# A convolution in Winograd form: the casting load of the last image pair split into 7, 65, 24 and 32 partitions

## Chip, core and metric

One core of one Trainium2 chip. The metric is the device time of one execution in microseconds (us); the median of the repeated runs is given, with lowest and highest in brackets. A ratio is the mean time of one kernel's fast runs over the mean of the other kernel's fast runs of the same rounds, so it is not quite the ratio of the medians quoted. The profiles name the engines of the core: PE multiplies matrices, DVE, ACT (ScalarE) and GpSimd (POOL) compute on elements, SP here only issues DMAs. A DMA is carried out by 16 DMA engines, which move packets and end each DMA with small completion packets (for the casting load of the kernel before 144 packets: 128 rows, and 16 of 4 bytes that take 9 ns in the median). The straggler, or late engine, is the DMA engine that ends last.

## The reference

A 3x3 convolution with padding 1, float32 in and out:

```python
batch, c_in, h, w, c_out = 16, 64, 64, 64, 128
x_pad = np.pad(x, ((0, 0), (0, 0), (1, 1), (1, 1)))
output[b, co] += weight[co, ci, kh, kw] * x_pad[b, ci, kh:kh+h, kw:kw+w]   # over ci, kh, kw
```

## The kernel before

Two images of 64 channels fill 128 partitions, so there are 8 pairs; each is 128 rows of 16 KB in float32. Seven pairs are loaded by plain DMAs from the SP queue into float32 tiles and cast to float16 by ScalarE or GpSimd. The last pair is cast during its load by one DMA from the GpSimd queue, the only queue in the kernel that casts. Each output pair is stored by two DMAs of 2 MB, the last pair by four of 1 MB.

Cut to the loads and stores, with some lines joined and `...` for what is left out:

```python
    def load(p):                                   # SP queue, float32
        xf[p] = next_slot([128, H, W], "xf")
        for lo, hi in cuts if p == 0 else [(0, H)]:
            keep(nc.sync.dma_start(
                    xf[p][:, lo:hi, :], x_rows[128 * p : 128 * p + 128, lo:hi, :]))
    ...
    def load_cast(p):                              # GpSimd queue, float32 -> float16
        xs[p] = xpool.tile([128, H, W], F16, tag="xc", name="xc")
        keep(nc.gpsimd.dma_start(xs[p], x_rows[128 * p : 128 * p + 128, :, :]))
    ...
    for p in range(NP):                            # NP = 8, NH = 7
        ...                                        # row sums of pair p + 1 on GpSimd
        if p == 0:
            for q in range(NH, NP):
                load_cast(q)
        for blk in range(4):
            ...                                    # matmuls, additions
            if blk in parts:                       # stores, SP queue
                for b2 in range(2):
                    keep(nc.sync.dma_start(out_rows[2 * p + b2, :, lo:hi, :], ...))
```

Of the kernel before, what the change touches and what calls it, by code (L numbers as in the profile page):

```python
# [13 lines left out]
def kernel(  # L14
# [6 lines left out]
    nc = tc.nc  # L21
# [6 lines left out]
    keep = tc.keep_in_program_order  # L28
    x_rows = x.rearrange("b c h w -> (b c) h w")
# [23 lines left out]
    xf, xs = {}, {}  # L53
# [23 lines left out]

    def load_cast(p):
        xs[p] = xpool.tile([128, H, W], F16, tag="xc", name="xc")
        keep(nc.gpsimd.dma_start(xs[p], x_rows[128 * p : 128 * p + 128, :, :]))  # L80

    for p in range(NH):
        load(p)
# [51 lines left out]
    for p in range(NP):  # L135
# [7 lines left out]
# [3 lines that stand above are left out]
# [92 lines left out]
```

## Time and profile before

| | before |
|---|---|
| time | 128.05 us (127.88 to 128.25, 3 runs) |
| span of the profiled execution | 126.0 us |
| last matmul / last addition end | 111 us / 113 us |
| bytes moved | 49.72 MB, of which 1.05 MB (as written) by the casting load |

The page of the profile has a line of 40 slices for each engine and for the DMA. The DMA line says how busy the engines were, and the GB/s line how much they moved: in the kernel after, at 24 us, the packets of the large loads took 904 ns in place of 624 and the DMA share stayed at 1.01, so an engine whose packets got longer still counts as busy. The stretch in which the casting load runs is shown here, as windows (columns: window, its length, busy us of PE, PE loads, DVE, ACT and GpSimd with instruction counts, granted clock, DMA share of 16 engines, GB/s as written), for the kernel before:

```profile
24.00:32.00 8.00, 8.00 (x76) 3.98 (x74) 6.46 (x11) 7.52 (x10) 2.47 (x2) 1.00 1.02 318
32.00:38.00 6.00, 6.00 (x60) 3.09 (x58) 4.58 (x8) 4.68 (x8) 4.21 (x2) 1.00 1.00 419
```

In the first window the rate is 318 GB/s at full share. That is no loss: half of the packets are cast rows (107 of 209), which read 16 KB and write 8 KB, and only what is written is counted (1.05 MB for the 128 rows; the page gives 17.07 MB read from HBM, which is all of the input in float32, 16.78 MB, and the weights). In the second the cast is nearly over and the rate is back.

### The profile page before, as it was taken

How to read it: one execution, taken by the hardware profiler on the slowest of the kernel's cores; microseconds unless marked ns; L12 is line 12 of the kernel's file. 1: busy time of each engine (PE TensorE's matmuls, PEld its weight loads, DVE VectorE, ACT ScalarE, POOL GpSimd, SP SyncE). 2: the span in 40 equal slices, each digit the busy share in tenths (PEclk: the TensorE clock that was granted, in tenths of full speed). 3: DMA queues.
4: the chain of work that ended last, by engine and by line, in shares of the span. 5: the costliest groups of instructions: out<-in, count | busy, mean ns of one | idle time of the engine just before them, and what ended most of it. 6: DMA issues, size and time to landing. Idle time of an engine off the chain costs nothing.

```text
span 126.0 us, 2439 instructions
## 1 busy us (share of the span) xinstructions
PE 106.0 (84%) x978; PEld 53.4 (42%) x978; DVE 84.4 (67%) x135; ACT 61.7 (49%) x94; POOL 33.6 (27%) x23
## 2 busy tenths in 40 slices
PE   0479999999999999999999999999999999940000
PEld 0334455545554545454545454555445544510000
DVE  0186777877777778777877787778777787770000
ACT  4184889998869896666333333333333333300000
POOL 2000297940661157005800480039000000000000
PEclk9999999999999999999999999999999999999555
DMA  4999999999999999999999999999999999999960
GB/s 122 304 431 443 427 426 426 348 320 317 393 432 427 429 429 427 421 432 421 437 437 416 442 416 432 437 421 421 432 421 437 437 416 442 413 406 437 429 265 13
DMA packets 4330, 49.72 MB, mean 395 GB/s; under 512 B 480, under 2 KB 480, under 8 KB 1120
## 3 DMA queue, kind: packets, MB, share of 16 engines
q1 hardware_dynamic: 4176, 48.53, 91.8%
q0 software_dynamic: 144, 1.05, 4.0%
q8 instruction: 7, 0.11, 0.3%
q14 instruction: 3, 0.02, 0.0%
HBM read 17.07 MB, written 33.55 MB: 402 GB/s over the span
## 4 chain that ended last, share of the span: by engine, by line
PE 82%; DMA 4%; DVE 2%; issue 1%; DVEq 0%; SPq 0%
PE acc L176 82%; DMA xf<-in_x_dram 4%; DVE ot L196 1%; DVE ss L98 1%; DVE ot L199 0%; DVEq L233 0%; SPq L51 0%; DVEq L196 0%
## 5 line engine op out<-in xcount | busy, mean ns | idle before, releaser
L176 PE MATMUL acc<-xs,Wt 64*128 64x504 f16 (+3 forms) x672 | 77.9, 379 | 0.0
L176 PEld LDWEIGHTS <-Wt 64*128 64x128 f16 x960 | 52.3, 95 | 53.7 <-issue 3.7
L196 DVE TENSOR_TENSOR ot<-acc,ut 128x512 f32<-128x512 f32 x64 | 41.3, 687 | 21.9 <-PE acc L176 19.0
L190 ACT COPY ut<-acc 128x512 f32<-128x512 f32 x64 | 34.4, 590 | 43.6 <-issue 39.0
L199 DVE TENSOR_TENSOR ot<-acc,ut 128x512 f32<-128x512 f32 x64 | 41.2, 685 | 0.2 <-PE acc L176 0.2
L176 PE MATMUL acc<-ss,Wt 64*128 64x504 f16 (+1 forms) x192 | 27.0, 384 | 1.6 <-DVE ss L98 1.6
L71 ACT CAST xs<-xf 128x1024 f16<-128x1024 f32 (+2 forms) x26 | 26.7, 1066 | 1.0 <-DMA xf<-in_x_dram 1.0
L98 POOL TENSOR_TENSOR ss<-xs 128x1024 f16<-128x1024 f16 x8 | 16.8, 2124 | 25.7 <-PE acc L176 25.7
L98 POOL TENSOR_TENSOR ss<-xf 128x1024 f16<-128x1024 f32 x4 | 9.4, 2370 | 14.2 <-DMA xf<-in_x_dram 14.2
L176 PE MATMUL acc<-xc,Wt 64*128 64x504 f16 (+3 forms) x96 | 10.9, 373 | 0.0
L98 POOL TENSOR_TENSOR ss<-xc 128x1024 f16<-128x1024 f16 x2 | 4.2, 2131 | 8.6 <-issue 8.6
L116 PE MATMUL wp<-ident,w 128*64 128x128 f16 x18 | 1.3, 328 | 4.2 <-DVE w L88 4.2
L98 DVE TENSOR_TENSOR ss<-xf 128x512 f16<-128x512 f32 x4 | 2.8, 690 | 2.9 <-DMA xf<-in_x_dram 2.9
L71 POOL CAST xs<-xf 128x896 f16<-128x896 f32 x2 | 1.9, 929 | 5.3 <-DMA xf<-in_x_dram 5.3
L88 DVE CAST w<-w_raw 128x576 f16<-128x576 f32 x1 | 0.5, 461 | 3.6 <-DMA w_raw<-in_weight_dram 3.6
L116 PEld LDWEIGHTS <-w 128*64 128x64 f16 x18 | 1.1, 209 | 4.2 <-DVE w L88 4.2
L118 ACT CAST Wt<-wp 128x384 f16<-128x384 f32 x1 | 0.5, 479 | 2.8 <-PE wp L116 2.8
L118 ACT ACT_TABLE_LOAD x1 | 1.3, 1283 | 0.7 <-PEq L222 0.7
L123 ACT CAST Wt<-wp 128x384 f16<-128x384 f32 x1 | 0.5, 478 | 0.5 <-DVE Wt L121 0.5
L80 POOL DMA_DIRECT2D xc<-in_x_dram x1 | 0.7, 694 | 0.0
L120 DVE TENSOR_TENSOR Wt<-wp,Wt 128x384 f16<-128x384 f32 x1 | 0.6, 550 | 0.0
L121 DVE TENSOR_TENSOR Wt<-wp,Wt 128x384 f16<-128x384 f32 x1 | 0.5, 548 | 0.0
(7 smaller groups left out, 1.4 us busy)
## 6 DMA issues: line engine op xcount, KB each, us to landing
out_dram<-ot SPq DMA_DIRECT2D x14, 2048.0 KB, 20.5
xf<-in_x_dram SPq DMA_DIRECT2D x6, 2048.0 KB, 26.5
out_dram<-ot SPq DMA_DIRECT2D x4, 1024.0 KB, 11.6
xf<-in_x_dram SPq DMA_DIRECT2D x2, 512.0 KB, 6.3
xc<-in_x_dram POOLq DMA_DIRECT2D x1, 1024.0 KB, 15.4
xf<-in_x_dram SPq DMA_DIRECT2D x1, 576.0 KB, 5.1
xf<-in_x_dram SPq DMA_DIRECT2D x1, 448.0 KB, 7.3
w_raw<-in_weight_dram SPq DMA_DIRECT2D x1, 288.0 KB, 2.9
```

The costliest lines, as they stand in the source:

```text
L71: keep(copy(xs[p][:, lo:hi, :], xf[p][:, lo:hi, :]))
L80: keep(nc.gpsimd.dma_start(xs[p], x_rows[128 * p : 128 * p + 128, :, :]))
L88: keep(nc.vector.tensor_copy(w16, w_raw))
L98: eng.tensor_add(ss[p][:, lo : lo + n, :], v[:, lo : lo + n, 0, :], v[:, lo : lo + n, 1, :])
L116: nc.tensor.matmul(wp[q : q + 64, k * CO : k * CO + CO], w16[:, t::9], ident)
L118: keep(nc.scalar.copy(wrow(G1), wps[1]))
L120: keep(nc.vector.tensor_sub(wrow(G21), wps[2], wrow(G1)))
L121: keep(nc.vector.tensor_sub(wrow(G01), wps[0], wrow(G1)))
L176: nc.tensor.matmul(tiles[b2][:, lo - j0 : hi - j0, c_lo:c_hi], Wt[p0 : p0 + 64, wi, kw, :], rhs, start=i == 0, stop=i == n - 1,)
L190: keep(nc.scalar.copy(ut, U[b2]))
L196: nc.vector.tensor_add(ots[p][b2][:, j0 : j0 + RB, 0, :], A[b2], us[b2])
L199: nc.vector.tensor_add(ots[p][b2][:, j0 : j0 + RB, 1, :], Bt[b2], us[b2])
```

## The change

The intent is to hand the rows of the casting load unevenly to the 16 DMA engines, so that an engine that is late at the end has fewer of them. The bytes are the same (1.05 MB).

```diff
-        keep(nc.gpsimd.dma_start(xs[p], x_rows[128 * p : 128 * p + 128, :, :]))
+        for a, b in ((0, 7), (7, 72), (72, 96), (96, 128)):
+            keep(nc.gpsimd.dma_start(xs[p][a:b], x_rows[128 * p + a : 128 * p + b, :, :]))
```

## The prediction

How the rows of the parts are shared among the engines was an assumption. The sum that rests on it is this. The late engine was taken to lose three rows of 0.624 us: 124.48 - 1.87 = 122.61 us. One of the latest others was taken to gain a row: 122.70 + 0.62 = 123.32 us. So the end moves by 1.16 us, and the time is 126.9 us. The rivals stand for other counts on the late engine: (a) a row more, (b) as many as before, (c) six fewer, with two more on others (127.5 us), or two more (129.3 us). The middle of these, drawn towards the first, was put at 127.2 us. The 0.6 us for an instruction fetch is the author's estimate from the 611 ns of a 16 KB packet; the seven fetch packets themselves took 882 to 1021 ns.

> **What bounds the kernel now.** I read the page first, for the busy shares and the slices, then the chain of waits, then the waits of the DMA-issuing queue (SP), then the DMA view of the last microseconds, and at last the single DMA packets that the trace records.
>
> ```profile
> span 126.0 us, 2439 instructions
> PE   0479999999999999999999999999999999940000
> DMA  4999999999999999999999999999999999999960
> q1 hardware_dynamic: 4176, 48.53, 91.8%
> q0 software_dynamic: 144, 1.05, 4.0%
> PE 82%; DMA 4%; DVE 2%; issue 1%; DVEq 0%; SPq 0%
> ```
>
> The reader is to see that DMA stands at 9 from the second slice to the last but two, while PE stops five slices before the end. The chain gives 82% to PE, and that is the trap: it is followed back from the last compute instruction it can tie, and its last piece, an addition on DVE, ends at 112.54 + 0.60 = 113.14 us, 12.9 us before the end. What lies in those 12.9 us is in the waits of the SP queue:
>
> ```profile
> SPq L204 <- DVE ot L199: 96.3, 18, 14.0
> SPq L233 <- DMA out_dram<-ot: 10.7, 3, 5.9
> ```
>
> At its last line the queue waits 10.7 us for stores to land. So the end is set by a backlog in the DMA engines, and PE's end would have to move by about 10 us before it mattered. The windows of the tail show how the backlog drains (columns: window, its length, busy us of five engines, clock, DMA share of 16 engines, GB/s):
>
> ```profile
> 118.00:121.00 3.00, 0.00 (x0) 0.00 (x0) 0.00 (x0) 0.00 (x0) 0.00 (x0) 0.50 1.00 423
> 121.00:122.00 1.00, 0.00 (x0) 0.00 (x0) 0.00 (x0) 0.00 (x0) 0.00 (x0) 0.50 0.56 238
> 122.00:122.50 0.50, 0.00 (x0) 0.00 (x0) 0.00 (x0) 0.00 (x0) 0.00 (x0) 0.50 0.43 180
> 122.50:123.00 0.50, 0.00 (x0) 0.00 (x0) 0.00 (x0) 0.00 (x0) 0.00 (x0) 0.50 0.08 33
> 123.50:124.00 0.50, 0.00 (x0) 0.00 (x0) 0.00 (x0) 0.00 (x0) 0.00 (x0) 0.50 0.08 33
> 124.00:124.30 0.30, 0.00 (x0) 0.00 (x0) 0.00 (x0) 0.00 (x0) 0.00 (x0) 0.50 0.06 27
> ```
>
> A share of 0.06 is one engine of 16. From 122.7 us to 124.5 us a single DMA engine works alone: a straggler. The packet records (start, duration, size, queue; no engine number) say the same: the 16 completion packets of the last store fall at 120.6, 120.8, 120.9, 121.1, 121.2, 121.3, 121.5, 122.0, 122.2, three at 122.3, 122.6, two at 122.7, and one at 124.48 us. Their mean is 121.94. The straggler is 1.78 us behind the next one (122.70). The same records, with packets chained by start = end of the one before, tell why: the usual 16 KB packet takes 611 ns, but on one engine, from 45.2 us to about 112 us, each takes 633 to 672 ns, so that a 2 MB store advances it by about 5.15 us against 4.86 us on the others, 13 times over: 3.8 us. Without that it would be among the earliest. Instruction fetch (seven packets of 16 KB) also delays some engines by about 0.6 us each and makes the second group at 122.0 to 122.7.
>
> The load to be changed is small:
>
> ```profile
> xc<-in_x_dram POOLq DMA_DIRECT2D x1, 1024.0 KB, 15.4
> L80 POOL DMA_DIRECT2D xc<-in_x_dram x1 | 0.7, 694 | 0.0
> ```
>
> Its 128 row packets (16 KB read, 8 KB written) take 624 ns each, eight to an engine, between 23.3 and 34.5 us, alternating with the large loads in the same engines.
>
> [...] in the stretch of the cast the two queues share the engines, 67.6% and 33.8%. So a row taken from an engine at 25 us lets its stores end one row-time sooner at 124 us, as long as it is never short of work. [...] The kernel before only has the 128-partition case (144 packets: 128 rows and 16 completions)[...]. [...] One slow engine is in this trace, about 5% on stores; its number is not recorded.
>
> **The change, part by part.** It removes one casting DMA on POOL and adds four, with 7, 65, 24 and 32 partitions. The order of instructions on the other engines is the same.
>
> POOL: three more issues at 694 ns are 2.1 us. They stand at 19.47 us, before additions that start at 20.85 us and take 4.69 us. The added issue ends at 22.2 us, so these end near 26.9 us instead of 25.5; PE needs them for the third pair, about 13 us per pair from 7.07 us, thus at 33 us. Cost on the path: nothing. The cast rows are read from 83.8 us on, some 50 us after landing: nothing.
>
> Bytes and rows: the same 128. Up to 48 more completion packets at 9 ns: 0.03 us per engine, nothing.
>
> [...] it ends at 124.48 - 1.87 = 122.61 us. The latest others, at 122.70, [...] end at 123.32. The end then moves from 124.48 to 123.32: minus 1.16 us, so 128.05 - 1.16 = 126.9 us.
>
> **The rivals.** (a) [...] it gets one row more, 128.05 + 0.62 = 128.7 us. [...] Against it: the relief of 1.87 us fits the lag of 1.78 us[...]. (b) [...] nothing changes, 128.05. (c) [...] the others set the end at 122.70 + 1.25 = 123.95, so 127.5 us; [...] 129.3 us. [...] (d) The slow rate is itself caused by the GpSimd path and moves to another engine with the split. Against it: the cast is over at 34.5 us and the slow packets begin at 45.2. (e) PE becomes the bound: no, it ends some 10 us before the last landing.
>
> **Range and chances.** The total work of the engines is conserved, so even a perfect balance could not end before the mean of 121.94: 2.54 us or 1.98% at the very best, and the split is coarse. A gain over 2% would need the slow engine to recover. A loss over 2% (2.6 us) would need four rows more on the straggler[...]. I give 0.55 to 126.9, 0.1 to no change, 0.2 to 128.7, 0.15 to rule (c). The middle of these, drawn towards the first, is 127.2 us; 126.5 to 128.8 holds the first four outcomes with the spread of the three runs (127.88 to 128.25).
>
> **What would show it.** In the changed profile: q0 with 128 row packets still of about 624 ns; a tail in which the window with a share of 0.06 is gone or shorter than 0.6 us, if the straggler was relieved; [...] the slow packets of about 645 ns still there on one engine. PE's last matmul and DVE's last addition should stay at 111 and 113 us. The prediction is wrong if the tail of one engine gets longer (rival a), [...] if the slow packets appear on more engines or vanish (rival d), or if PE stalls on the pair that the cast feeds.

## The result and the profile after

| | before | after |
|---|---|---|
| time | 128.09 us (127.88 to 128.25, 4 runs) | 132.16 us (131.92 to 132.86, 4 runs) |
| ratio of the fast runs | | 1.0327, 95% interval 1.0285 to 1.037 |
| span | 126.0 us | 130.3 us |

The changed kernel is 3.3% slower; the prediction was 127.2 us with a range to 128.8. From the page of the kernel after, the lines that answer to those of the prediction:

```profile
span 130.3 us, 2447 instructions
PE   0499999999996999999999999999999999600000
DMA  4999999999999999999999999999999999999950
GB/s 129 295 446 448 407 438 438 292 259 299 231 241 400 435 428 412 433 443 417 433 438 428 417 433 433 433 412 433 438 417 433 433 417 425 435 420 415 428 241 13
q1 hardware_dynamic: 4176, 48.53, 91.6%
q0 software_dynamic: 224, 1.05, 4.0%
PE 79%; DMA 4%; DVE 2%; ACT 1%; issue 1%; DVEq 0%; SPq 0%
```

The DMA line is as full as before, and the bytes are the same. But the GB/s line has a trough of five slices, 292 259 299 231 241, from about 23 to 39 us, where the kernel before has 348 320 317 and then 393. That is where the time went: engines that are busy and move less. Its windows:

```profile
24.00:32.00 8.00, 8.00 (x77) 3.99 (x75) 6.55 (x12) 7.35 (x11) 3.19 (x3) 1.00 1.01 280
32.00:38.00 6.00, 6.00 (x60) 3.12 (x58) 4.58 (x8) 2.89 (x5) 4.13 (x2) 1.00 0.99 228
```

280 in place of 318 GB/s, and 228 in place of 419, at a DMA share of 1.01 and 0.99. In the later stretch the two are alike again (428 and 429 GB/s from 46 to 110 us). The SP queue's wait at its last line and the tail:

```profile
SPq L236 <- DMA out_dram<-ot: 14.7, 4, 7.5
```

```profile
126.00:127.00 1.00, 0.00 (x0) 0.00 (x0) 0.00 (x0) 0.00 (x0) 0.00 (x0) 0.50 0.20 82
127.00:128.00 1.00, 0.00 (x0) 0.00 (x0) 0.00 (x0) 0.00 (x0) 0.00 (x0) 0.50 0.08 33
128.00:129.00 1.00, 0.00 (x0) 0.00 (x0) 0.00 (x0) 0.00 (x0) 0.00 (x0) 0.50 0.04 16
```

The wait grew from 10.7 to 14.7 us, by the 4 us of the loss, and a lone engine (a share of about 0.06) is still there at the end: the completions stand at 126.69, 127.34 and 128.75 us. PE has a small stall in slice 13, because ACT got loads late (it waited 3.7 us for one, to 39.7 us), but DVE's last addition still ends at 114.0 us, some 15 us ahead of the last landing.

The single packets of the trace (start, duration, size, queue) show what a busy but slow engine is. I sorted the 16 KB packets of the large loads by time:

```
large-load packets of 16 KB, mean (lowest) duration in ns; cast rows beside them, mean
              before                 after
24 to 25 us   624 (624)  cast 624    904 (812)   cast 624
28 to 29 us   624 (624)  cast 624    857 (792)   cast 624
33 to 34 us   611 (611)  cast 819*  1077 (1021)  cast 645
36 to 37 us   611 (611)  -          1034 (976)   cast 669
40 to 41 us   611 (611)  -           612 (611)   -
(* a single one, delayed by an instruction fetch)
```

So the cast rows themselves take nearly what they took, and the large load packets beside them take 1.4 to 1.8 times their former time in the mean, for 16 us (195 of the 210 that start between 23.1 and 39.7 us took over 690 ns). Added up, the time over 624 ns of the packets that took over 690 ns is 3.75 us for each of the 16 engines (before: 0.07 us, from instruction fetches).

### The profile page after: what moved, and what is told of

Same layout as the page of the kernel before. It is cut to its first block, busy times and chain, and to the rows that moved or that the text cites. A ratio compares the mean times of both kernels' runs of the same rounds, so it can differ in the third digit from the quotient of the medians.

```text
span 130.3 us, 2447 instructions
## 1 busy us (share of the span) xinstructions
PE 106.2 (81%) x978; PEld 55.2 (42%) x978; DVE 84.2 (65%) x135; ACT 61.5 (47%) x94; POOL 35.2 (27%) x26
## 3 DMA queue, kind: packets, MB, share of 16 engines
q0 software_dynamic: 224, 1.05, 4.0%
## 4 chain that ended last, share of the span: by engine, by line
PE 79%; DMA 4%; DVE 2%; ACT 1%; issue 1%; DVEq 0%; SPq 0%
PE acc L179 79%; DMA xf<-in_x_dram 4%; ACT ut L193 1%; DVE ot L199 1%; DVE ss L101 1%; DVE ot L202 0%; DVEq L236 0%; ACT xs L71 0%; SPq L51 0%; DVEq L199 0%
## 5 line engine op out<-in xcount | busy, mean ns | idle before, releaser
L179 PE MATMUL acc<-xs,Wt 64*128 64x504 f16 (+3 forms) x672 | 80.9, 377 | 1.2 <-ACT ut L193 1.1
L179 PEld LDWEIGHTS <-Wt 64*128 64x128 f16 x960 | 54.1, 95 | 53.0 <-issue 4.7
L179 PE MATMUL acc<-ss,Wt 64*128 64x504 f16 (+1 forms) x192 | 30.8, 384 | 1.3 <-DVE ss L101 1.3
L71 ACT CAST xs<-xf 128x1024 f16<-128x1024 f32 (+2 forms) x26 | 26.8, 1069 | 4.4 <-DMA xf<-in_x_dram 4.4
L179 PE MATMUL acc<-xc,Wt 64*128 64x504 f16 (+3 forms) x96 | 11.6, 373 | 0.0
L83 POOL DMA_DIRECT2D xc<-in_x_dram x4 | 2.2, 562 | 0.0
```

The source lines that it names most:

```text
L71: keep(copy(xs[p][:, lo:hi, :], xf[p][:, lo:hi, :]))
L83: keep(nc.gpsimd.dma_start(xs[p][a:b], x_rows[128 * p + a : 128 * p + b, :, :]))
L179: nc.tensor.matmul(tiles[b2][:, lo - j0 : hi - j0, c_lo:c_hi], Wt[p0 : p0 + 64, wi, kw, :], rhs, start=i == 0, stop=i == n - 1,)
```

## Experiments

Three theories. **Place**: DMAs over 7, 65, 24 or 32 neighbouring partitions lengthen the packets of the large loads beside them, and DMAs whose partitions are spread over all 128 do not. The packet records name neither engine nor partition, so no trace here shows a reason, and the runs test only the statement itself. A range that follows a cut, up to late_split, is what this theory gave, unless told otherwise. **Count**: four software DMAs with their completions slow the engines. **Imbalance**: the uneven row counts alone make some engines late. The line in each diff is the one in `load_cast`, unless told otherwise.

**free4: four DMAs, each over all 128 partitions.**

```diff
+        for a, b in ((0, 16), (16, 32), (32, 48), (48, 64)):
+            keep(nc.gpsimd.dma_start(xs[p][:, a:b, :], x_rows[128 * p : 128 * p + 128, a:b, :]))
```

> The casting load is cut into 4 DMAs too, but along the image rows, so that each still spans all 128 partitions [...]. [...] no slow packets, large loads beside it stay near 624 ns per 16 KB, time 128.0 to 128.8 us. Count theory (four software DMAs and their extra completions slow the engines): large loads of 800 to 1100 ns and about 131 to 132 us.

Measured: 128.19 us (127.89 to 128.49), ratio 1.0002 (0.9954 to 1.0049). Large loads beside the cast stayed at 624 ns. Four software DMAs cost nothing: the count theory falls. (The cast itself stretched over a longer time, 20.1 us in the median from issue to landing in place of 15.4, as its packets, 512 in place of 128, are a quarter in size and alternate one by one with the large ones.)

**half2: two contiguous halves, even row counts.**

```diff
+        for a, b in ((0, 64), (64, 128)):
+            keep(nc.gpsimd.dma_start(xs[p][a:b], x_rows[128 * p + a : 128 * p + b, :, :]))
```

> The casting load is cut into partitions 0 to 63 and 64 to 127: two DMAs, four rows on each of 16 engines, so 8 rows per engine as before. [...] large loads of 800 to 1100 ns while the cast lasts and 130 to 133 us. Imbalance theory (the uneven row counts alone cost the 4 us): 128.1 us, as the counts are even. Count theory: a third of the loss, about 129.4 us.

Measured: 129.69 us (129.25 to 129.96), ratio 1.0107 (1.0051 to 1.0164). A little under the range that the place theory gave, but 102 large-load packets took over 690 ns, with a median of 862 ns, and their excess is 1.53 us per engine, which is the loss of 1.6 us. By the counts every engine had 8 rows (160 packets on the software queue: 128 rows and 16 completions for each half, none over), so imbalance is not needed for a loss. The windows:

```profile
24.00:32.00 8.00, 8.00 (x78) 4.02 (x76) 5.95 (x10) 7.52 (x11) 2.97 (x2) 1.00 1.01 287
32.00:38.00 6.00, 6.00 (x62) 3.00 (x58) 4.58 (x9) 4.68 (x8) 4.21 (x2) 1.00 1.01 317
```

**eight16: eight DMAs of 16 partitions, even row counts.**

```diff
+        for a, b in [(i, i + 16) for i in range(0, 128, 16)]:
+            keep(nc.gpsimd.dma_start(xs[p][a:b], x_rows[128 * p + a : 128 * p + b, :, :]))
```

> The casting load at its old place, cut into eight DMAs of 16 partitions: one row per engine each, so 8 rows per engine in all, no imbalance. [...] worse than the two halves (plus 1.6 us[...]), so slow large loads of well over 1000 ns and 131 to 136 us. Theory that only the uneven counts [...] matter: 128 to 129.7 us.

Measured: 134.05 us (132.76 to 134.69), ratio 1.0458 (1.0387 to 1.0529). With 16 partitions to a DMA in place of 64, 235 packets took over 690 ns, with a median of 1111 ns. Its windows:

```profile
24.00:32.00 8.00, 8.00 (x78) 4.01 (x74) 6.24 (x10) 7.53 (x11) 5.60 (x3) 1.00 1.07 230
32.00:38.00 6.00, 6.00 (x60) 3.10 (x58) 4.58 (x9) 3.63 (x6) 4.22 (x2) 1.00 0.99 225
```

The rate is worse than the changed kernel's in the first window (230 against 280) although the row counts are even.

**stride2: two DMAs, the even partitions and the odd ones.** The first range is for the place theory; the second is for the case that any split by partitions slows the loads.

```diff
+        for a in (0, 1):
+            keep(nc.gpsimd.dma_start(xs[p][a::2], x_rows[128 * p + a : 128 * p + 128 : 2, :, :]))
```

> The casting load at its old place as two DMAs of 64 partitions, the even ones and the odd ones: four rows per engine each[...]. [...] near the kernel before, 128.0 to 128.8 us, large loads near 624 to 700 ns. [...] as the two contiguous halves, about 129.7 us.

Measured: 127.82 us (127.60 to 128.11), ratio 0.9985 (0.9958 to 1.0013). Large loads at 624 ns. The windows:

```profile
24.00:32.00 8.00, 8.00 (x78) 4.02 (x74) 6.54 (x11) 7.35 (x11) 2.84 (x3) 1.00 1.02 325
32.00:38.00 6.00, 6.00 (x62) 3.07 (x58) 4.58 (x9) 4.76 (x8) 3.80 (x2) 1.00 1.01 421
```

These are the rates of the kernel before. Two DMAs of 64 partitions each, as in half2, and the same count of 160 packets, as in half2; only the partitions are spread over all 128. So it is not the size of the DMA or the number of engines that slows the loads, but which partitions each DMA takes, as the place theory says. The time is a little under the expected range, as is that of late_whole below.

**loadhalf: a plain load cut in halves, the casting load untouched.** In `load`:

```diff
+            for a, b in ((0, 64), (64, 128)) if p == 5 else [(0, 128)]:
+                keep(nc.sync.dma_start(
+                        xf[p][a:b, lo:hi, :], x_rows[128 * p + a : 128 * p + b, lo:hi, :]))
```

> No change to the casting load; in its place one plain float32 load of 2 MB (the sixth pair) is cut into two halves of 64 partitions on the hardware queue, counts even. [...] packets up to twice 611 ns for 8 rows, so plus 3 to 5 us, 131 to 133 us. If the slowing needs the software queue or the cast: 128.1 us.

Measured: 133.88 us (133.15 to 134.00), ratio 1.0445 (1.0408 to 1.0482). That is slower than the range expected. 181 packets took over 690 ns, with a median of 1224 ns: twice 611. No software queue is needed, and the cast was over at 34.8 us, while the slow packets go on to about 46 us. 64 partitions at a time cost this load half its rate: 16 KB in 1224 ns are 13.4 GB/s for an engine, in 611 ns 26.8. The window in which the halves run, after the cast:

```profile
38.00:44.00 6.00, 6.00 (x59) 3.45 (x57) 3.75 (x7) 5.56 (x8) 0.00 (x0) 1.00 1.02 217
```

The five together with the two kernels, with the excess of the large-load packets over 624 ns per engine, from the packet records of 22 to 56 us of one execution, beside the difference in time:

| kernel | packets over 690 ns | their excess per engine, us | time against before, us |
|---|---|---|---|
| before | 3 | 0.07 | 0 |
| free4 | 4 | 0.09 | +0.1 |
| stride2 | 3 | 0.07 | -0.2 |
| half2 | 102 | 1.53 | +1.6 |
| after | 198 | 3.75 | +4.1 |
| loadhalf | 181 | 6.65 | +5.9 |
| eight16 | 235 | 7.20 | +6.1 |

The excess accounts for the time in each, to about 1 us.

Two things limit the place theory. First, a rival stands untested: neighbouring partitions are also neighbouring rows in DRAM, and every run that changed the one changed the other. Against it, a cast row reads as many bytes as a large packet (16 KB) and writes half, and in eight16 the cast rows took 647 ns in the mean, beside large packets of 1111 ns; that is a hint, not a test. Second, it does not say how the delay spreads: in eight16 229 of the 230 large packets that start beside the cast took over 690 ns, although each part covers only 16 of the 128 partitions. How the delay reaches nearly all of them is not shown.

**late_whole and late_split: the same load and the same split, beside stores.** The last large load lands at about 45 us in the kernel before, and at about 40 us when the cast comes later. Issued at the fourth pair, the cast runs from about 54 us, beside stores, which read the memory that loads write. In the expectation of late_split the range after the second cut is for the case that packets lengthen beside stores as they do beside loads.

```diff
-        if p == 0:
+        if p == 3:
             for q in range(NH, NP):
                 load_cast(q)
```

> The whole 128-partition casting load, issued at the fourth pair (about 50 us) in place of the first, when the large loads are over and only stores run. A control for late_split. The work of each engine is the same, so both theories: 127.8 to 128.5 us.

> The split into 7, 65, 24 and 32 of the changed kernel, issued at about 50 us beside stores, which read the partitions rather than write them. [...] the slow packets are nearly gone, and what is left is the imbalance that was predicted: minus 1.2, 0 or plus 0.6 us against late_whole, depending on the straggler's place. [...] again plus 3 to 4 us. Count theory: plus 3 to 4 us.

Measured on the same chip: late_whole 127.68 us (127.40 to 127.81), ratio 0.9959 (0.9913 to 1.0004); late_split 128.94 us (128.89 to 129.07), ratio 1.0061 (1.0017 to 1.0106). Beside stores the split leaves nearly all packets at 611 to 624 ns: from 53 to 68 us none of 261 store packets took over 690 ns in late_whole and 4 of 260 in late_split, 0.12 us of excess per engine in place of 3.75. So beside stores the packets lengthen far less than beside loads. They are not wholly free of it: in the five other uneven runs below, 16 to 22 of about 250 store packets took over 690 ns, an excess of 0.36 to 0.45 us per engine. Of the 4.1 us, the split keeps 1.26 us here. The prediction had allowed minus 1.2, 0 or plus 0.6. The tail of late_whole, and then that of late_split:

```profile
123.00:124.00 1.00, 0.00 (x0) 0.00 (x0) 0.00 (x0) 0.00 (x0) 0.00 (x0) 0.50 0.10 41
124.00:125.00 1.00, 0.00 (x0) 0.00 (x0) 0.00 (x0) 0.00 (x0) 0.00 (x0) 0.50 0.00 0
```

```profile
122.00:123.00 1.00, 0.00 (x0) 0.00 (x0) 0.00 (x0) 0.00 (x0) 0.00 (x0) 0.50 0.54 229
123.00:124.00 1.00, 0.00 (x0) 0.00 (x0) 0.00 (x0) 0.00 (x0) 0.00 (x0) 0.50 0.20 82
124.00:125.00 1.00, 0.00 (x0) 0.00 (x0) 0.00 (x0) 0.00 (x0) 0.00 (x0) 0.50 0.06 25
125.00:126.00 1.00, 0.00 (x0) 0.00 (x0) 0.00 (x0) 0.00 (x0) 0.00 (x0) 0.50 0.04 16
```

From 124.1 to 125.65 us one engine works alone: the straggler is still there, and not relieved.

**Three other orders of the same parts, late.** The author assumed that the order decides which engines get fewer rows. No trace shows that; the first range is for a late engine that gets fewer rows, the last for one that does not.

```diff
+        for a, b in ((0, 65), (65, 89), (89, 96), (96, 128)):   # late_65_24_7
+        for a, b in ((0, 7), (7, 31), (31, 96), (96, 128)):     # late_7_24_65
+        for a, b in ((0, 24), (24, 89), (89, 96), (96, 128)):   # late_24_65_7
```

> The late split with the parts in the order 65, 24, 7, 32. [...] The order 7, 65, 24 cost 1.26 us against the late whole load (127.68 us). If the straggler is now light: 127.5 to 128.2 us, one engine's tail gone [...]. [...] 128.3 to 129.0 us, with a lone engine in the tail.

> The late split in the order 7, 24, 65, 32. [...] the time is 127.3 to 128.1 us, about that of the late whole load or a little under. Else 128.3 to 129.0 us.

> The late split in the order 24, 65, 7, 32: [...] 127.3 to 128.1 us and no lone engine in the tail. Else 128.3 to 129.0 us.

Measured: 128.77 us, ratio 1.0060 (1.0030 to 1.0089); 128.67 us, ratio 1.0055 (1.0031 to 1.0078); 128.75 us, ratio 1.0055 (1.0034 to 1.0077), all against the kernel before. None helps; the lone engine is in the tail of each.

**Other sizes, late.** By the same assumption, the three ranges of each expectation are for a late engine that gets fewer rows, a row more, or as many as before.

```diff
+        for a, b in ((0, 27), (27, 92), (92, 112), (112, 128)):   # late_27_65_20_16
+        for a, b in ((0, 20), (20, 85), (85, 112), (112, 128)):   # late_20_65_27_16
```

> The late split with other sizes: 27, 65, 20, 16. [...] it is now 1.25 us earlier: 127.5 to 128.1 us and no lone engine in the tail. [...] 128.6 to 128.9 us; [...] 127.7 to 128.3 us but with the lone engine still in the tail.

> The same sizes in the order 20, 65, 27, 16: [...] 127.5 to 128.1 us again, no lone engine in the tail. [...] 128.6 to 128.9 us; [...] 127.7 to 128.3 us with a lone engine.

Measured: 128.51 us, ratio 1.0058 (1.0037 to 1.0079), and 128.53 us, ratio 1.0055 (1.0040 to 1.0071). Again no help. Both times lie 0.4 us above the range for a late engine with fewer rows (up to 128.1 us).

**late_half2: even counts, late.** The halves of half2 at the late place.

> The two halves of 64 partitions, late, beside stores: even counts[...]. If uneven counts are all that the late splits lose by: as the late whole load, 127.4 to 128.1 us. If splitting as such costs, at any place: 128.4 to 128.9 us.

Measured: 127.66 us (127.42 to 127.78), ratio 0.9983 (0.9961 to 1.0006). No loss: at the late place splitting as such costs nothing, uneven shares do. Only the six uneven ones lose. (Their long packets are a part of that: 0.36 to 0.45 us per engine in five of them, 0.12 in late_split, 0.02 in late_half2.)

Why the late engine is not relieved can be read from its packets. It is the one whose 16 KB stores take 633 to 672 ns, so it can be followed through the cast as a chain in which each packet starts where the one before ends, with completion packets between the DMAs. This is a reconstruction from times, as the records have no engine number:

```
cast rows on the slow engine, by DMA (start in us)
late_whole         54.4 55.6 56.9 58.1 59.3 60.5 61.8 62.4                                  8 rows
late_split         53.7 | 54.9 56.1 57.4 58.6 59.8 | 61.7 62.9 | 64.1 65.3       1+5+2+2 = 10 rows
late_7_24_65       54.6 | 56.4 57.6 | 59.5 60.7 61.3 62.5 63.8 | 65.6 66.8       1+2+5+2 = 10 rows
late_27_65_20_16   53.9 55.1 | 56.9 58.2 59.4 60.6 61.8 | 63.1 64.3 | 66.1       2+5+2+1 = 10 rows
```

Two rows more are 1.25 us, the loss of late_split. As a check, its stores from the completion at 48.51 us on to its end at 125.65 take 77.14 us; in late_whole the same number from 47.92 to 124.09 takes 76.17. The difference of 0.97 us, plus about 0.25 for six fewer slow packets, is 1.2 us again.

The traces say more than this. If a packet is taken as the next one of an engine only where it starts 3 or 4 ns before the end of a store, or 18 to 20 ns before the end of a cast row (the usual steps here), every chain from the last slow packet before the cast to the first one after it has 10 cast rows in five of the six uneven runs, and 8 in late_whole, late_whole5 and late_half2; in late_65_24_7, 10 or 8 fit. So the order of the parts changed nothing for this engine.

The 4-byte packets of the software queue fit these rows. Even DMAs leave 16 each: 16 in the kernel before, 64 in free4, 32 in half2, 128 in eight16. The four uneven ones leave 96, not 64. If each of the 16 engines has as many places in every DMA as the slow engine has rows, the parts 7, 65, 24 and 32 make 16 x (1+5+2+2) = 160 places for 128 rows; 32 stay empty, and 64 + 32 = 96. The parts 27, 65, 20 and 16 make 16 x (2+5+2+1) = 160 too, and 96 were counted. For these parts that is the number of partitions over 16, rounded up. In late_split three engines can be seen to write such packets in turn with stores, every 0.61 us, one of them 11 times from 53.44 to 59.59 us: the 1+5+2 empty places and 3 completions of the first three parts.

**late_whole5: the late whole load with more rounds.**

> The late whole load again, with more rounds, as control of the two orders and as the candidate to beat the kernel before. It was 0.4% faster with an interval that just touched none. [...] 127.5 to 128.1 us.

Measured: 127.79 us (127.41 to 128.40, 6 runs), ratio 0.9982 (0.9957 to 1.0007). It beats the changed kernel, but against the kernel before the interval contains 1. No run here is clearly faster than the kernel before.

## Why the prediction was wrong

- **Right: what bounds the kernel.** The end is the drain of the DMA backlog. Work on the DMA engines 100 us before the end came back in full at the end: 3.75 us of lost engine time at 23 to 39 us in the profile, 4 us more waiting in the last line of the SP queue. (PE stops a little over four slices before the end, not five; nothing rests on it.)
- **Right: GpSimd, PE and the completions cost nothing.** free4 with as many issues took 128.19 us. The four issues of the changed kernel took 2.2 us, 1.5 more than the one before (2.1 was estimated). There were 80 more small packets (224 - 144) and not 48; they took 9 to 34 ns, 0.09 us for each engine with the 16 from before, which is still nothing.
- **The step that failed: the price of a row, with the late engine relieved by 3 x 0.624 = 1.87 us, and "The total work of the engines is conserved".** It priced a row at 624 ns on whatever engine and moved only the count. The cast rows did take about that, 634 ns in the mean. But the packets of the large loads beside them went from 624 to between 850 and 1100 ns in the mean. DMAs of neighbouring partitions go with it (medians of 862 ns in half2, 1111 in eight16), and DMAs over spread partitions (free4, stride2: 624 ns) do not; why is not shown. The prediction's bound of 1.98% on a gain may stand, but its "a loss over 2% would need four rows more on the straggler" does not: the engines can lose time together. None of the rivals named this.
- **The second step that failed: the assumed sharing of the rows, and with it that the late engine "ends at 124.48 - 1.87 = 122.61 us".** Beside stores, where the long packets are few, the late engine got two rows more, not three fewer. The forecast's sharing, which no trace showed, left no engine with 10 rows; that of rival (c) put two more on some, and its estimate for the late engine among them was plus 1.25 us (129.3): late_split measured 1.26 us over late_whole. The count of 96 small packets fits it too. So rival (c), given 0.15, had the late engine's rows right. The three engines of late_split that write the 1+5+2 empty places keep only the 2 rows of the last part by this count, so they should be light by 6 rows, 3.7 us; in late_split three stop together at 119.8 us, 2.1 us ahead of the next. A part of their lead was lost on the way: at 99 to 100.3 us some engines were without work, 1.7 us of engine time in all, and none in late_whole.
- **Rival (d) is not what happened:** the slow engine's packets are there in every profile, with about 630 to 690 ns, on one engine, from 40 to 50 us (its first stores) to 111 to 116 us.
- **What stays open.** How the 4.1 us divide in the changed kernel itself. The long packets are measured (3.75 us per engine), and so is the cost of the split beside stores (1.26 us); the two sum to 5.0, so they overlap, and in the crowded stretch the rows of each engine cannot be counted. That the packets are long because of the neighbouring partitions, and not because of the neighbouring rows in DRAM, is not tested; nor is it shown how the delay reaches nearly all engines. What makes the one engine slow at stores is not found either: in the kernel before it is slow from about 45 to 112 us, when no software DMA runs, and in late_whole its packets are at 624 ns just while the software DMA runs beside its stores (54 to 63 us).

## What to carry to other kernels

A DMA over part of the partitions was not a smaller DMA over all of them here: beside loads, halves lengthened packets of the large loads from 624 ns to a median of 862 (half2), and parts of 16 partitions to one of 1111 (eight16), while beside stores halves cost nothing (late_half2: 127.66 us, 0.02 us of excess). So before splitting by partitions, ask which partitions each part takes and what else is moving beside it at that time; split along the free dimension or by a stride if it must be split (128.19 and 127.82 us, no loss). When the DMA share stays full and the GB/s line sinks with the same mix of transfers, look for packets that got longer, not for more packets (here 280 and 228 GB/s in place of 318 and 419, at a share of 1.0). To balance engines, first measure how many rows the late engine really gets: the number of small packets on the queue (96 in place of 64 here) can tell of uneven shares before any time is read.
